# Normalised operand splits, convolutions read from PSUM, batched attention sums and a new planner clock rule in a two-layer hybrid encoder

## The chip, the cores and the metric

The kernel runs as one program on one core of a Trainium2 chip. The metric is the device time of one execution in microseconds (us); lower is better. Engines are named as in the profile: PE is TensorE (matmuls), DVE is VectorE, ACT is ScalarE, POOL is GpSimd and SP issues the DMAs. PSUM is the memory that PE writes, in eight banks of 128x512 float32; SBUF holds everything else.

## The reference

What is computed is an encoder of two layers on 512 tokens of width 1024, all in float32:

```python
def reference(x, positions, norm_mix, w_in, ...):
    for l in range(DEPTH):
        h = rms_norm(x, norm_mix[l])
        proj = h @ w_in[l]
        aq, ak, av, dqkv, dz, dalpha, dbeta, rwp = _split(proj, IN_SPLITS)
        y_att = attention_mixer(aq, ak, av, positions, attn_sink[l])
        y_dn = deltanet_mixer(dqkv, dz, dalpha, dbeta, dn_conv[l], dn_a_log[l],
                              dn_dt_bias[l], dn_norm[l])
        y_rw = rwkv_mixer(rwp, rw_mu[l], rw_w0[l], rw_w_up[l], ...)
        mixed = jnp.concatenate([y_att, y_dn, y_rw], axis=-1)
        x = x + mixed @ w_out[l]
        h = rms_norm(x, norm_ffn[l])
        x = x + conv_ffn(h, ffn_w_up[l], ffn_conv[l], ffn_w_down[l])
    return rms_norm(x, norm_final)
```

`rms_norm` divides each token by the root mean square of its 1024 values and multiplies by a gain. The attention mixer has six query heads, two key/value heads, a window of 128 tokens to either side, a rotation of part of each head (rope) and a sink per head. The DeltaNet mixer runs a width-5 convolution along the tokens, then a chunked recurrence with a triangular inverse in each of the two directions. The RWKV mixer mixes each token with its two neighbours (token shift) and runs a chunked recurrence in both directions. `conv_ffn` is a gated feed-forward net with a width-3 convolution between its two products.

## The kernel before

Activations lie transposed: 128 features in the partitions, 512 tokens along a row, so that x is eight tiles of 128x512. Every large product is made in a split form: a float32 operand a is written as ah + al, both in PE's faster 32-bit type, and `product` (line 738) issues three matmuls for each of the eight k-tiles: wh by xh, wh by xl and wl by xh. A projection is thus 24 matmuls of 512 columns into one PSUM bank. For its weights `weights` loads four k-tiles at a time by DMA into `wr`, ACT casts them into `wh`, and POOL subtracts, `wl` = `wr` - `wh`.

A layer has a mixer part with 26 projections: eight for RWKV, one for the DeltaNet gates, nine for the DeltaNet convolutions, three for its output gates, and K, V and three Q for attention. Around them stand `rwkv_prep` (twice), `invert` (a forward substitution on 32x32 blocks, 30 dependent steps on DVE), `finish_inverse`, `rwkv_scan` (eight steps), `dn_prep` (three times), `invert_both` (30 steps on DVE), `dn_scan` (eight steps), three attention heads, `rwkv_out` and `dn_out`. Then follow the output projection `w_out`, the feed-forward up-products (44 tiles) and the down-products (eight tiles of 22 k-tiles).

The norm is put in late. `split` takes x times its gain only, and the factor of each token, 1/rms, lies as a row tile `rb` (128x512). Each consumer multiplies the projection's PSUM result by `rb`: `token_shift` (line 889), `dn_conv` (line 1103), `dn_gates`, `rope`, the V tile and `gate_proj`. In `dn_conv` that multiplication also moves the result from PSUM into an SBUF tile `td`; four DVE instructions then add the shifted taps, reading `td`:

```python
V.tensor_tensor(u, o, rb, mult)
S.activation(dst, u, AF.Copy, scale=w(2))
```

An attention head works through four blocks of 128 queries, and in each on two groups: scores, maximum, exponential, the sum `den`, its reciprocal, a scaling, transposes and the product with V. The small instructions (`es`, `nmx`, `den`) are 128x2 in size, once in each block.

The order of all work is decided when the program is built. The class `Plan` records each instruction with its price and its dependencies; `schedule` then runs a list scheduler over the five engines, in which an instruction's priority is the longest path behind it plus a lead for its task from the table `LEAD` (37 numbers, the same for both layers). Some instructions have an alternative engine (`other`, line 268): copies may go to ACT or DVE, though not those that write the matmul's split type. The program is emitted in the order of the planned starts, and all of its instructions carry the line of that one call, L516. An instruction waits on the chip for its operands, and the queue behind it waits with it.

## Time and profile before

| what | us |
|---|---|
| median of three runs | 1678.78 |
| the three runs | 1677.74 to 1680.12 |
| the profiled execution, its own time | 1681.65 |
| its span | 1679.5 |
| PE busy | 1531.1 |
| DVE busy | 1083.1 |
| ACT busy | 736.2 |
| POOL busy | 645.2 |
| mixer part of layer 0 (from the first matmuls to the end of `dn_out`) | 13 to 434 |
| `w_out` of layer 0 | 434 to 480 |
| feed-forward part of layer 0 | 480 to 840 |
| the same three of layer 1 | 840 to 1260, 1260 to 1306, 1306 to 1664 |

The page gives each engine's busy time, the granted clock of PE in 40 slices, the chain of work that ended last, and groups of instructions by shape. The busy time of PE has to be read with care: matmul records overlap, and a matmul that runs at the lower clock lasts longer. Because every instruction carries the same line, the groups are told apart by tile names and shapes: `td`, `tr` and `cv` are working tiles in SBUF, `ps` is PSUM, `hh` and `hl` are the two halves of an activation, `wh` and `wl` those of a weight, `rb` is the norm's factor and `fixed` holds constants and parameters.

### The profile page before, as it was taken

To read this page: it belongs to the slowest core of one execution; us is meant where nothing else is said; L and a number is where in the kernel's file an instruction comes from. 1 tells how busy PE (TensorE), PEld (TensorE's weight loads), DVE (VectorE), ACT (ScalarE), POOL (GpSimd) and SP (SyncE) were. 2 spreads that over 40 slices of the span, in tenths; PEclk is the share of its full clock that TensorE was granted. 3 is DMA by queue.
4 is the path that set the end of the run, shared out by engine and by line. 5 is a ranking of instruction groups with operands and counts; after the bars stand their busy time and mean duration, and the time that the engine had idled before them with its cause. 6 is when DMAs were issued, how large, how long until landed. Compare 5 with 4: busy or idle time off the path is not lost. (4 is left out here: it accounts for less than half of the span.)

```text
span 1679.5 us, 29012 instructions
## 1 busy us (share of the span) xinstructions
PE 1531.1 (91%) x11500; PEld 1192.8 (71%) x11500; DVE 1083.1 (64%) x1689; ACT 736.2 (44%) x1399; POOL 645.2 (38%) x510
## 2 busy tenths in 40 slices
PE   7999787589999999999999996966899999999996
PEld 5677665367777777788876775644677877777885
DVE  7799977967437666740058998789654566766101
ACT  5565345454543433332236544355544433334221
POOL 5422332010555554555552232410017454555553
PEclk9999889779999999999999997996799999999998
DMA  6312303010233333333342121120003333333332
GB/s 177 84 34 76 70 20 89 13 34 2 71 91 100 94 89 95 94 106 112 108 105 64 47 75 39 54 86 1 27 14 89 94 88 95 95 93 88 115 91 85
DMA packets 230536, 126.07 MB, mean 75 GB/s; under 512 B 23656, under 2 KB 221416, under 8 KB 230400
## 3 DMA queue, kind: packets, MB, share of 16 engines
q1 hardware_dynamic: 228624, 121.02, 25.8%
q10 hardware_dynamic: 1776, 3.20, 0.7%
q8 instruction: 90, 1.47, 0.3%
q14 instruction: 46, 0.38, 0.1%
HBM read 117.84 MB, written 6.34 MB: 74 GB/s over the span
## 5 line engine op out<-in xcount | busy, mean ns | idle before, releaser
L516 POOL TENSOR_TENSOR wl<-wr,wh 128x512 fp32r<-128x512 f32 (+1 forms) x408 | 558.1, 1379 | 830.1 <-ACT wh L516 667.9
L516 PE MATMUL ps<-hh,wh 128*128 128x512 f32 x1248 | 457.6, 399 | 6.9 <-ACT wh L516 6.9
L516 ACT ACTIVATE wh<-wr 128x512 fp32r<-128x512 f32 (+1 forms) x408 | 243.5, 616 | 495.9 <-PE ps L516 433.9
L516 PE MATMUL ps<-hh,wl 128*128 128x512 f32 x1248 | 452.9, 398 | 7.4 <-POOL wl L516 5.3
L516 PE MATMUL ps<-hl,wh 128*128 128x512 f32 x1248 | 451.6, 394 | 0.0
L516 PEld LDWEIGHTS ps<-hh,wl 128*128 128x128 f32 x1248 | 232.7, 187 | 84.2 <-POOL wl L516 30.3
L516 PEld LDWEIGHTS ps<-hh,wh 128*128 128x128 f32 x1248 | 233.6, 188 | 69.8 <-ACT wh L516 16.2
L516 PEld LDWEIGHTS ps<-hl,wh 128*128 128x128 f32 x1248 | 233.8, 188 | 51.7 <-issue 3.4
L516 DVE TENSOR_TENSOR p<-ps,p 128x512 f32<-128x512 f32 (+2 forms) x72 | 38.2, 551 | 197.4 <-PE ps L516 197.1
L516 PE MATMUL ps<-p,wh 128*128 128x512 f32 x512 | 158.2, 389 | 0.0
L516 DVE TENSOR_TENSOR td<-ps,rb 128x512 f32<-128x512 f32 (+1 forms) x64 | 43.7, 688 | 136.4 <-PE ps L516 136.3
L516 PEld LDWEIGHTS ps<-p,wh 128*128 128x128 f32 x512 | 96.1, 188 | 19.9
L516 DVE SCALAR_TENSOR_TENSOR tr<-td,fixed,tr 128x511 f32<-128x511 f32 x88 | 105.3, 1197 | 0.6 <-ACT tr L516 0.4
L516 PE MATMUL ps<-p,wl 128*128 128x512 f32 x256 | 99.8, 390 | 0.0
L516 ACT ACTIVATE p<-p 32x256 f32<-32x256 f32 (+3 forms) x112 | 66.0, 589 | 16.1 <-DVE p L516 11.2
L516 PE MATMUL ps<-fixed,cv 128*128 128x128 f32 x168 | 36.6, 338 | 38.8 <-ACT cv L516 35.7
L516 DVE SCALAR_TENSOR_TENSOR td<-tr,fixed,td 128x511 f32<-128x511 f32 x88 | 70.8, 805 | 0.3
L516 PE MATMUL ps<-p,p 32*32 32x32 f32 (+2 forms) x1232 | 56.1, 253 | 14.9 <-DVE p L516 11.3
L516 DVE TENSOR_TENSOR tr<-tr,td 128x512 f32<-128x512 f32 x44 | 67.3, 1529 | 1.6
L516 ACT ACTIVATE p<-ps 64x256 f32<-64x256 f32 (+4 forms) x113 | 44.9, 401 | 52.7 <-PE ps L516 33.3
L516 PEld LDWEIGHTS ps<-sm,p 64*64 64x64 f32 x1344 | 49.4, 145 | 24.6 <-DVE sm L516 12.9
L516 PEld LDWEIGHTS ps<-p,p 32*32 32x32 f32 (+1 forms) x1232 | 51.3, 143 | 21.5 <-DVE p L516 12.1
(170 smaller groups left out, 2089.5 us busy)
## 6 DMA issues: line engine op xcount, KB each, us to landing
wr<-ffn_w_up SPq DMA_DIRECT2D x176, 256.0 KB, 2.8
wr<-w_in SPq DMA_DIRECT2D x88, 256.0 KB, 2.8
wr<-ffn_w_down SPq DMA_DIRECT2D x80, 256.0 KB, 2.9
p<-scr ACTq DMA_DIRECT2D x12, 256.0 KB, 5.1
wr<-w_in SPq DMA_DIRECT2D x24, 128.0 KB, 2.6
wr<-w_out SPq DMA_DIRECT2D x32, 96.0 KB, 2.6
wr<-w_out SPq DMA_DIRECT2D x16, 192.0 KB, 2.6
p<-xt SPq DMA_DIRECT2D x8, 256.0 KB, 4.5
```

What stands on the lines that cost most here:

```text
L516: tc.keep_in_program_order(call(*args, **kw))
```

## The change

The eight RWKV projections keep the late norm, now applied in place in PSUM. After each of them `renorm` makes one k-tile of the normalised input (x times gain times `rb`, on DVE) and splits it anew into `gh` and `gl`; all other 18 projections of the mixer take this split, and their consumers lose the multiplication by `rb`. `dn_conv` reads its taps from PSUM. `rope` makes its scaled copy on ACT and both products on DVE, and `gate_proj` takes its sigmoid from PSUM. An attention head now holds all eight score tiles and makes `es`, `nmx`, `den` and the reciprocal once, at 128x8; its parts have leads of their own. In the planner, casts that write the split type may move from ACT to DVE, and products and sums of two SBUF tiles may move between DVE and POOL; the `LEAD` table has an entry for each task in each layer; and the rule by which the planner prices PE's clock is another. The feed-forward code is as it was, and so is the number of instructions on PE.

```diff
...
@@ LEAD @@
-    "attn_head0": -17500, "attn_head1": 13500, "attn_head2": 4300, ...
...
@@ def other @@
-        if not self.flexible or not writes or len(reads) < 1 or "float32r" in str(writes[0].dtype) or reads[0].dtype != F32:
+        if not writes or not reads:
             return None
...
+        if name == "tensor_tensor" and not psum and n >= 128 and len(dst.shape) == 2 and o.eng in ("DVE", "POOL"):
+            e, f, cost = ("POOL", self.nc.gpsimd, 180 + 2.3 * n) if o.eng == "DVE" else ("DVE", self.nc.vector, 165 + 1.04 * n)
+            return e, f.tensor_tensor, o.args, o.kw, cost
...
@@ def split @@
-        hi = plan.tile(bp, [P, T], F32R, tag=f"hh{k}", bufs=2, name=nm("hh"))
+        hi = plan.tile(bp, [P, T], F32R, tag=f"{tag}h{k}", bufs=1, name=nm(tag + "h"))
...
@@ def token_shift @@
-        u = t2("r")
+        u = o
         V.tensor_tensor(u, o, rb, mult)
...
@@ def dn_conv @@
-    def dn_conv(l, o, i, rb, dst):
-        u = t2("d")
-        V.tensor_tensor(u, o, rb, mult)
+    def dn_conv(l, u, i, dst):
...
@@ def rope @@
-        V.scalar_tensor_tensor(q, o, scale, rb, mult, mult)
+        S.activation(q, o, AF.Copy, scale=scale)
+        V.scalar_tensor_tensor(dst, o, scale, cos_t, mult, mult)
         pr = ps("r")
         PE.matmul(pr, C("rot"), q, start=True, stop=True)
-        V.tensor_tensor(dst, pr, sin_t, mult)
-        G.tensor_tensor(q, q, cos_t, mult)
+        V.tensor_tensor(q, pr, sin_t, mult)
         V.tensor_tensor(dst, dst, q, add)
...
@@ def attn_head @@
+        V.tensor_tensor(den, den, es, add)
+        V.reciprocal(den, den)
+        po = ps("r")
...
@@ def layer @@
+        def renorm(k):
+
+            xn = t2("d")
+            V.scalar_tensor_tensor(xn, x[k], norm.g[:, k : k + 1], rb, mult, mult)
+            normed.append(split(xn, None, "g", k))
...
-            o = proj(l, parts, COL_RW + P * i)
+            o = proj(l, parts, COL_RW + P * i, st="jjod"[i % 4])
...
+            renorm(i)
...
+        parts = normed
...
-            V.tensor_tensor(z, o, rb, mult)
-            sigmoid(sg, z)
-            V.tensor_tensor(z, z, sg, mult)
+            sigmoid(sg, o)
+            V.tensor_tensor(z, o, sg, mult)
...
-                o = proj(l, parts, COL_DQKV + P * i)
+                o = proj(l, parts, COL_DQKV + P * i, st="o" if i == pr_ < 2 else "j")
                 dst = cv()
-                dn_conv(l, o, i, rb, dst)
+                dn_conv(l, o, i, dst)
...
```

What the planner makes of it is shown at three places, each before and after. The first is DVE at the first DeltaNet convolutions of layer 0, behind `rwkv_prep` (`cv` is a convolution's result, `td` the normalised copy). Before:

```order
98 L516 TENSOR_TENSOR td_254<-ps_246,rb_75 128x512
99 L516 TENSOR_TENSOR td_264<-ps_256,rb_75 128x512
100 L516 SCALAR_TENSOR_TENSOR p_276<-fixed,p_276 128x512
101 L516 SCALAR_TENSOR_TENSOR cv_253<-td_254,fixed,cv_253 128x510
102 L516 COPY fixed<-ps_245 128x8x6
103 L516 SCALAR_TENSOR_TENSOR cv_263<-td_264,fixed,cv_263 128x510
104 L516 SCALAR_TENSOR_TENSOR cv_253<-td_254,fixed,cv_253 128x511
105 L516 SCALAR_TENSOR_TENSOR cv_263<-td_264,fixed,cv_263 128x511
106 L516 SCALAR_TENSOR_TENSOR cv_253<-td_254,fixed,cv_253 128x511
107 L516 SCALAR_TENSOR_TENSOR cv_263<-td_264,fixed,cv_263 128x511
108 L516 SCALAR_TENSOR_TENSOR cv_253<-td_254,fixed,cv_253 128x510
109 L516 SCALAR_TENSOR_TENSOR cv_263<-td_264,fixed,cv_263 128x510
```

After:

```order
111 L547 TENSOR_SCALAR cv_278<-ps_271,fixed 128x512
112 L547 TENSOR_TENSOR p_221<-ps_247,fixed 128x512
113 L547 SCALAR_TENSOR_TENSOR cv_278<-ps_271,fixed,cv_278 128x510
114 L547 SCALAR_TENSOR_TENSOR cv_278<-ps_271,fixed,cv_278 128x511 x2
115 L547 SCALAR_TENSOR_TENSOR cv_278<-ps_271,fixed,cv_278 128x510
116 L547 SCALAR_TENSOR_TENSOR p_289<-fixed,p_289 128x512
117 L547 CAST wh_339<-wr_338 128x512
118 L547 SCALAR_TENSOR_TENSOR td_260<-fixed,td_260 12x512
119 L547 TENSOR_TENSOR cv_278<-cv_278,td_279 128x512
```

The copies into `td` (rows 98 and 99 of before) are gone, the taps read `ps`, and a weight cast stands among them (row 117), which ACT did before.

The second place is PE at the end of `dn_scan` in layer 0 (`sm` is the scan's state and vectors, `hh` and `hl` with `wh` the first matmuls of `w_out`, `at` with `at` the scores of attention, `tr` with `at` its product with V). Before:

```order
1193 L516 MATMUL ps_799<-sm_798,p_388 64x64 x4
1194 L516 MATMUL ps_799<-sm_798,p_529 64x64 x4
1195 L516 MATMUL ps_799<-sm_798,p_544 64x64 x4
1196 L516 MATMUL ps_815<-p_383,sm_779 64x64 x2
1197 L516 MATMUL ps_815<-p_385,sm_797 64x64 x2
1198 L516 MATMUL ps_850<-hh_828,wh_852 128x512
1199 L516 MATMUL ps_861<-hh_828,wh_863 128x512
1200 L516 MATMUL ps_813<-sm_800,cv_253 64x64 x4
1201 L516 MATMUL ps_813<-sm_800,cv_331 64x64 x4
1202 L516 MATMUL ps_813<-sm_800,cv_398 64x64 x4
1203 L516 MATMUL ps_815<-p_524,sm_779 64x64 x2
```

After:

```order
1186 L547 MATMUL ps_752<-p_548,sm_751 64x64 x2
1187 L547 MATMUL ps_771<-at_443,at_515 128x256
1188 L547 MATMUL ps_772<-at_443,at_515 128x256
1189 L547 MATMUL ps_791<-td_790,fixed 128x512
1190 L547 MATMUL ps_821<-hh_799,wh_823 128x512
1191 L547 MATMUL ps_832<-hh_799,wh_834 128x512
1192 L547 MATMUL ps_821<-hl_800,wh_823 128x512
1193 L547 MATMUL ps_832<-hl_800,wh_834 128x512
1194 L547 MATMUL ps_821<-hh_799,wl_824 128x512
1195 L547 MATMUL ps_832<-hh_799,wl_835 128x512
1196 L547 MATMUL ps_794<-td_793,fixed 128x512
1197 L547 MATMUL ps_797<-td_796,fixed 128x512
1198 L547 MATMUL ps_703<-tr_718,at_463 64x128
1199 L547 MATMUL ps_703<-tr_720,at_463 64x128
1200 L547 MATMUL ps_703<-tr_718,at_463 64x128
```

Before, 16 matmuls of `w_out` stand among the scan's last matmuls and another 16 beside `dn_out`, and no attention work is left by then. After, none stands inside the scan and six beside `dn_out`; behind them come the last attention head's remaining 20 transposes and 34 products with V (rows 1198 on), and the rest of `w_out` after those.

The third place is DVE in the up-products of layer 0's feed-forward part. Before:

```order
641 L516 TENSOR_TENSOR td_1028<-ps_1021,rb_848 128x512
642 L516 TENSOR_TENSOR tr_1018<-ps_1011,rb_848 128x512
643 L516 TENSOR_SCALAR td_1019<-tr_1018,fixed 128x512
644 L516 SCALAR_TENSOR_TENSOR tr_1029<-td_1028,fixed,tr_1029 128x511
645 L516 SCALAR_TENSOR_TENSOR td_1019<-tr_1018,fixed,td_1019 128x511
646 L516 SCALAR_TENSOR_TENSOR tr_1029<-td_1028,fixed,tr_1029 128x511
647 L516 SCALAR_TENSOR_TENSOR td_1019<-tr_1018,fixed,td_1019 128x511
648 L516 TENSOR_TENSOR tr_1010<-tr_1010,td_1019 128x512
649 L516 TENSOR_TENSOR p_1020<-tr_1010,p_1020 128x512
```

After:

```order
699 L547 CAST p_1067<-tr_1057 128x512
700 L547 TENSOR_TENSOR p_1067<-tr_1057,p_1067 128x512
701 L547 CAST wh_1101<-wr_1100 128x512
702 L547 CAST wh_1108<-wr_1107 128x512
703 L547 TENSOR_TENSOR td_1094<-ps_1087,rb_819 128x512
704 L547 TENSOR_TENSOR tr_1084<-ps_1077,rb_819 128x512
705 L547 SCALAR_TENSOR_TENSOR tr_1095<-td_1094,fixed,tr_1095 128x511
706 L547 SCALAR_TENSOR_TENSOR td_1085<-tr_1084,fixed,td_1085 128x511
707 L547 SCALAR_TENSOR_TENSOR tr_1095<-td_1094,fixed,tr_1095 128x511
708 L547 SCALAR_TENSOR_TENSOR td_1085<-tr_1084,fixed,td_1085 128x511
709 L547 TENSOR_TENSOR tr_1076<-tr_1076,td_1085 128x512
710 L547 CAST p_1086<-tr_1076 128x512
```

The work on `ps` and `td` is the same, and casts of weights (`wh`) and of the result (`p` from `tr`), which ACT made before, now stand between: 41 weight casts and 14 others in each layer's up-products.

## Rows read from the trace of the kernel before

**Rows 1.** The page's parts 1 and 2: busy time of each engine; granted clock in tenths.

```profile
PE 1531.1 (91%) x11500; PEld 1192.8 (71%) x11500; DVE 1083.1 (64%) x1689; ACT 736.2 (44%) x1399; POOL 645.2 (38%) x510
...
PEclk9999889779999999999999997996799999999998
```

**Rows 2.** Busy time by stretch (us; x is instructions), then granted clock, DMA share, GB/s.

```profile
13.00:73.00 60.00, 57.51 (x237) 41.62 (x238) 45.98 (x55) 28.45 (x53) 29.00 (x21) 1.00 0.41 105
80.00:146.00 66.00, 61.83 (x815) 50.21 (x813) 61.18 (x86) 43.99 (x89) 13.75 (x8) 1.00 0.20 54
146.00:203.00 57.00, 46.15 (x309) 37.18 (x303) 54.81 (x85) 21.62 (x40) 22.24 (x17) 0.90 0.32 75
203.00:210.00 7.00, 5.42 (x140) 4.80 (x140) 4.91 (x12) 4.35 (x11) 0.00 (x0) 0.50 0.01 2
210.00:265.00 55.00, 49.03 (x686) 37.18 (x687) 39.00 (x74) 19.95 (x38) 20.28 (x27) 0.92 0.11 27
265.00:298.00 33.00, 24.36 (x231) 16.20 (x231) 28.29 (x48) 21.70 (x43) 2.50 (x5) 0.90 0.37 94
298.00:346.00 48.00, 29.59 (x125) 18.15 (x123) 44.92 (x102) 20.26 (x59) 2.59 (x3) 0.72 0.04 11
362.00:380.00 18.00, 15.63 (x224) 11.61 (x221) 9.02 (x30) 7.10 (x20) 1.68 (x2) 0.70 0.11 39
480.00:740.00 260.00, 257.44 (x1108) 205.95 (x1107) 172.16 (x198) 101.69 (x160) 132.02 (x93) 1.00 0.32 92
```

**Rows 3.** Groups of DVE instructions by shape: busy us, mean ns, then idle before.

```profile
L516 DVE SCALAR_TENSOR_TENSOR cv<-td,fixed,cv 128x511 f32<-128x511 f32 x36 | 30.9, 885 | 0.7
...
L516 DVE SCALAR_TENSOR_TENSOR p<-tr,fixed,p 128x511 f32<-128x511 f32 x32 | 30.4, 952 | 1.3 <-ACT p L516 0.4
...
L516 DVE SCALAR_TENSOR_TENSOR cv<-td,fixed,cv 128x510 f32<-128x510 f32 x36 | 27.8, 785 | 1.8 <-ACT cv L516 1.4
...
L516 DVE TENSOR_TENSOR td<-ps,rb 128x512 f32<-128x512 f32 x62 | 42.4, 689 | 136.4 <-PE ps L516 136.3
...
L516 DVE TENSOR_TENSOR cv<-cv,td 128x512 f32<-128x512 f32 x24 | 23.8, 1006 | 5.8 <-ACT td L516 5.7
...
L516 DVE TENSOR_SCALAR td<-tr,fixed 128x512 f32<-128x512 f32 x40 | 21.8, 544 | 1.4
...
L516 DVE TENSOR_TENSOR p<-p,tr 128x512 f32<-128x512 f32 x18 | 13.2, 739 | 1.3 <-ACT tr L516 0.7
...
L516 DVE SCALAR_TENSOR_TENSOR p<-p,fixed,rb 128x512 f32<-128x512 f32 x8 | 5.4, 745 | 5.6 <-ACT rb L516 5.6
...
L516 DVE TENSOR_TENSOR es<-fixed,mx 128x2 f32<-128x2 f32 x24 | 4.6, 191 | 0.7
```

**Rows 4.** DVE beside POOL in the feed-forward stage: start us, duration us, engine, operation.

```profile
617.74 0.51 DVE L516 TENSOR_SCALAR td<-tr,fixed 128x512 f32<-128x512 f32 x1
618.17 1.78 DVE L516 SCALAR_TENSOR_TENSOR tr<-td,fixed,tr 128x511 f32<-128x511 f32 x1
619.87 0.74 DVE L516 SCALAR_TENSOR_TENSOR td<-tr,fixed,td 128x511 f32<-128x511 f32 x1
...
616.66 2.73 POOL L516 TENSOR_TENSOR wl<-wr,wh 128x512 fp32r<-128x512 f32 x2 [0.47 <-PE ps L516]
```

**Rows 5.** DVE at four steps of the DeltaNet scan, layer 0, same columns as rows 4.

```profile
367.65 0.56 DVE L516 TENSOR_TENSOR sm<-ps,fixed 128x384 f32<-128x384 f32 x1 [3.04 <-PE ps L516]
...
380.32 0.55 DVE L516 TENSOR_TENSOR sm<-ps,fixed 128x384 f32<-128x384 f32 x1
...
408.52 0.56 DVE L516 TENSOR_TENSOR sm<-ps,fixed 128x384 f32<-128x384 f32 x1 [0.16 <-PE ps L516]
...
414.26 0.56 DVE L516 TENSOR_TENSOR sm<-ps,fixed 128x384 f32<-128x384 f32 x1 [1.11 <-PE ps L516]
```

**Rows 6.** PE, attention work between steps of the same scan, same columns as rows 4.

```profile
405.73 0.66 PE L516 MATMUL ps<-fixed,cv 128*128 128x128 f32 x4
406.32 1.31 PE L516 MATMUL ps<-tr,at 128*64 128x128 f32 x14
```

More of the change, by code (lines that the diff above doesn't have):

```diff
@@ L120 @@
 LEAD = {
[6 rows of a table removed]
-    "token_shift": 631900,
[20 rows of a table added]
 }
@@ L273, in other @@
         n = int(np.prod(dst.shape[1:]))
-        psum = str(src.space).endswith("PSUM")
+        psum = any(str(x.space).endswith("PSUM") for x in reads + writes)
         if o.eng == "ACT" and name == "activation" and o.args[2] == AF.Copy and set(o.kw) <= {"scale"}:
@@ L329, in price @@
         return n
-    SWITCH, STAY, COLD, WARM = 150, 300, 5000, 4000
+    SWITCH, STAY = 150, 300
+    BEAT, DOWN, UP = 3413.0, 0.44, 0.8
+    WEIGHT = {"full": 1.0, "half": 0.8, "q64": 0.9, "q32": 0.2}
     def admit(self, t):
@@ L385, in schedule @@
         avail = {e: [] for e in engines}
-        last, cold, heat, dma_free, releases = None, False, 0.0, 0.0, []
+        last, slow, here, then, edge, lit, dma_free, releases = None, False, 0.0, 0.0, self.BEAT, 0.0, 0.0, []
         push, pop = heapq.heappush, heapq.heappop
@@ L405, in wake @@
         def wake(r, t):
-            for h, e in held[r]:
-                push(heaps[e], (max(t, h.ready), h.n))
-            held[r] = []
+            was, held[r] = held[r], []
+            for h, e in was:
+                if h.done:
+                    continue
+                still = blocked(h)
+                if still is None:
+                    push(heaps[e], (max(t, h.ready), h.n))
+                else:
+                    held[still].append((h, e))
         order = []
@@ L483, in schedule @@
                 last = o.mode
-                if t - free[e] > self.COLD:
-                    cold, heat = True, 0.0
-                if cold:
+                while t >= edge:
+                    slow = here < (self.UP if slow else self.DOWN) * self.BEAT
+                    here, then, edge = then, 0.0, edge + self.BEAT
+                if slow:
                     cost *= 2
-                    heat += cost if o.mode == "full" else 0
-                    cold = heat < self.WARM
-            elif o.contend and e == "DVE" and free["POOL"] > t:
+                w, a, b = self.WEIGHT[o.mode], max(t, lit), t + cost + 150
+                if b > a:
+                    here += w * max(0.0, min(b, edge) - a)
+                    then += w * max(0.0, b - max(a, edge))
+                    lit = b
+            elif e == "DVE" and (o.contend or o.eng == "POOL") and free["POOL"] > t:
                 cost += min(cost, free["POOL"] - t)
@@ L1299, in attn_head @@
     def attn_head(l, tq, q, k, vt, dst):
[L1300 to L1304 removed]
+        span = [(max(0, nb - 1), min(3, nb + 1) + 1) for nb in range(4)]
+        scs = [[cv() for g in range(2)] for nb in range(4)]
+        mxt, nmx, es, den = (tiny(8, tag=tag) for tag in ("mx", "nmx", "es", "den"))
+        by = lambda a: a.rearrange("p (n g) -> p n g", g=2)
+        for nb, (k0, k1) in enumerate(span):
+            W = P * (k1 - k0)
             m0 = P * (k0 - nb + 1)
[L1306 to L1307 removed]
             for g in range(2):
@@ new lines, in attn_head @@
+        yield
+        V.tensor_tensor(by(es), sinkb[l][:, tq : 6 : 3].unsqueeze(1).broadcast_to([P, 4, 2]), by(mxt), sub)
+        V.tensor_scalar(nmx, mxt, -1.0, None, mult)
+        S.activation(es, es, AF.Exp)
+        for nb, (k0, k1) in enumerate(span):
+            W = P * (k1 - k0)
+            for g in range(2):
+                u = slice(2 * nb + g, 2 * nb + g + 1)
+                S.activation(scs[nb][g][:, :W], scs[nb][g][:, :W], AF.Exp, bias=nmx[:, u], accum_out=den[:, u])
+        yield
```

76 lines of the change are left out of this document (32 added, 44 removed), and 26 rows, old and new, of the table LEAD.

## The prediction

> **What bounds the kernel now.** I first read the page's busy times and the granted clock in slices [rows 1], then busy time by stretch [rows 2], then the DVE groups by shape [rows 3], then single instructions at three places [rows 4 to 6]. The chain of waits is no help here, as it covers only the end of the run. PE is busy 91% of the span [rows 1], but the stretches differ. In the feed-forward stretch, PE works 257.44 of 260 us at full clock while DVE works 172.16 [rows 2]: PE sets that time, and 257.44 us over 1108 instructions is 0.232 us for one split matmul. The first projections (13 to 73) are alike, PE 57.51 of 60. In the mixer it is DVE that is full: 61.18 of 66 us, 54.81 of 57, and 44.92 of 48 in the last forward substitution [rows 2]. PE looks busy beside it, but its clock stands at 0.90, 0.72 and 0.70 of full in these stretches, that is, part of the time at 1.2 instead of 2.4 GHz. It lies low after PE had little to do: in 298 to 346 PE works 29.59 of 48 us. In the two scans, short steps run from PE to DVE and back, and nothing is full. So a microsecond taken from PE in the mixer is worth little, one taken from DVE much, and in the feed-forward part neither DVE nor ACT matters until one reaches PE's time.
>
> **The change, part by part.** I laid the two orders of DVE side by side, cut them at the same tasks, and priced each instruction at its mean in this trace. In layer 0 and layer 1 this gives, before and after: `rwkv_prep` with the first convolutions 67.0 to 64.8 and 68.1 to 59.1; `invert` to `finish_inverse0` 58.9 to 58.0 and 58.3 to 55.9; `rwkv_scan` with `dn_prep` 75.7 to 60.4 and 75.2 to 64.3; `invert_both` with its `finish_inverse` 60.9 to 58.1 and 60.9 to 59.9; `dn_scan` 44.4 to 34.8 and 44.4 to 33.9; the end up to `dn_out` 5.8 to 11.9 and 5.8 to 15.5.
>
> Where this comes from, per layer: nine multiplications by `rb` into `td` fall away, 9 x 0.689 = 6.2 us [rows 3], and four of V and the gates. The 36 taps of the convolutions go from 0.885 and 0.785 [rows 3] to reading PSUM, where the 0.689 of `td<-ps,rb` is the nearest row: 36 x 0.146 = 5.3. The 16 token shifts save 16 x (0.952 - 0.689) = 4.2. Nine sums `cv<-cv,td` at 1.006 and nine `p<-p,tr` at 0.739 go to POOL (15.7). Nine in twelve of each tiny attention instruction go; `es` at 0.191 is the row for them. Added are eight `renorm` (nearest row `p<-p,fixed,rb`, 0.745: 6.0), three `gl`, some 18 weight casts and up to 13 copies from PSUM of half width. For the cast the trace has no row on DVE; the nearest is the copy with a scale, `td<-tr,fixed`, 0.544 [rows 3], so 18 x 0.544 = 9.8. Bounds for a cast: 0.51 [rows 4] below, 1.78, a fully held instruction in rows 4, above. I take 0.544, as a cast has the same one input.
>
> By stage, what of this lies on the path:
>
> First projections: PE is the bound; `renorm` and its splits add some 10 us to DVE's 45.98 of 60 [rows 2], less the 4.2 of token shift. Hidden: 0. Without that cover it would cost the 10.
>
> 80 to 146, DVE full: -2.2 in layer 0, -9.0 in layer 1. A convolution now holds its PSUM bank for five reads instead of one, 3.4 us instead of 0.7. The next projection needs 24 x 0.232 = 5.6 us in another bank, which covers that: 0, at worst 2.7 for each of nine.
>
> 146 to 210, DVE full: -0.9 and -2.4. In layer 1 the fill of split matmuls (97 instead of 175 during `invert`) leaves 26 for the inside of `finish_inverse0`, a 7 us stretch at clock 0.50 with PE at 5.42 [rows 2]; at full clock half of that goes: -2.5 in layer 1, bounds 0 and -2.7 each.
>
> 210 to 298: DVE loses 15.3 and 10.9, but it was busy only 39.00 of 55 and 28.29 of 33 us, and PE 49.03 and 24.36 [rows 2]. PE receives K, V and Q projections that stood elsewhere: by counts, 8.1 us more work in layer 0 and 15.5 in layer 1. The next late thing is PE. Bounds are -15.3 and +8.1 (layer 1: -10.9 and +15.5); I take -2.5 and 0, near PE's side, since the waits between engines remain.
>
> 298 to 362, DVE nearly full: -2.8 and -1.0, from the attention pieces leaving the gaps between substitution steps.
>
> `dn_scan`: the `t1` instructions of DVE mark the steps, at 367.65, 380.32, 408.52 and 414.26 [rows 5]. The first step shown takes 12.7 us, the last 5.7, and from 367.65 to 414.26 there are six steps in 46.6 us. The long one carries attention work on both engines at clock 0.70 (362 to 380, [rows 2]). With DVE's 44.4 at 34.8 and one attention head out of the way, I set all steps to 6.3: 37.8 instead of 46.6, -8.8 in each layer. Bounds 0 and -12 (all at 5.7).
>
> After the scan: before, 32 matmuls of `w_out` were done by the end of `dn_out`, now 6. The other 26 come later, 26 x 0.232 = +6.0 in each layer; beside `dn_out` now stands the end of the last head: 20 transposes at 0.66 / 4 and 34 products at 1.31 / 14 [rows 6], 6.5 us of PE. That is cover of the same size as the matmuls were, and not a second cost. Bounds 0 and +14, if the head's chain through DVE and ACT outlasts it.
>
> Feed-forward: 59 more casts on DVE in each layer, 59 x 0.544 = 32, so 172.16 becomes 204 of 257 [rows 2]. ACT is relieved and was not the bound. 0.
>
> The sum is -11.2 in layer 0 (-2.2 -0.9 -2.5 -2.8 -8.8 +6.0) and -17.7 in layer 1 (-9.0 -2.4 -2.5 -1.0 -8.8 +6.0), together -28.9. The profiled execution took 1681.65, which gives 1652.7. The median lies 2.87 below that execution, so I forecast 1650.
>
> **One rule against this change.** In rows 4 POOL works on two `wl` from 616.66 to 619.39. The scaled copy on DVE at 617.74 takes 0.51 all the same, while the instruction with two SBUF inputs at 618.17 takes 1.78, ending after POOL does, and its like at 619.87 takes 0.74. So an input from PSUM or one SBUF input goes free, and two are held. The Trainium skill, page "SBUF — State Buffer", section "Who interferes with whom", says that a DVE instruction with two SBUF inputs contends with POOL's reads, and the trace agrees (0.74 against 1.78). It also says that copies, casts and scaled copies can take both ports and then contend; the 0.51 does not show that here. By that rule a cast would be held like the 1.78 above.
>
> **The rivals.** *Slower: POOL holds DVE.* POOL gets 24 more two-input instructions per layer, in the stretches where DVE is full. Each can hold a two-input instruction of DVE, 1.78 - 0.74 = 1.04 us [rows 4]: 48 x 1.04 = 50 us in all. On top, if casts are held as well, the feed-forward DVE stands at 172 + 41 x 1.5 + 18 x 0.544 = 243, near PE's 257, with order waits on weights perhaps 4 us per layer. The forecast's 28.9 is lost when 0.6 of each possible hold occurs; at all of them the time is 1650 + 50 = 1700. For it: the 1.006 of `cv<-cv,td`, against 0.739 for `p<-p,tr`, shows holds in the mixer already. Against it: POOL works only 13.75 of 66 us and 2.50 of 33 in these stretches [rows 2], so most new work falls where nobody is held, and the taps now read PSUM and cannot be held. 0.17.
>
> *Same: PE takes back what DVE gives.* If the projections moved into 210 to 298 are not covered, this stage costs +8.1 and +15.5 instead of -2.5 and 0: 1650 + 26 = 1676. For it: PE's 49.03 of 55 us. Against it: a fifth of PE's time there is at the lower clock. 0.11.
>
> *Much faster: the clock stays up.* By rows 2 the time at the lower level in layer 0 is twice the missing share: 11 of 57 us, 7 of 7, 9 of 55, 7 of 33, 27 of 48, 11 of 18, together 72 us. If the moved fill keeps PE working and half of this time hangs on PE, each layer saves a further 72 / 2 / 2 = 18: 1650 - 36 = 1614. For it: PE gets more fill under `invert_both` (58 and 72 split matmuls of the gates). Against it: in `invert` it gets less, and under the substitutions the path is DVE's. 0.12.
>
> **How the numbers follow.** The forecast has 0.60; its own range is 1626 (all of DVE's saving in 210 to 298 counts) to 1668 (the head's chain outlasts `dn_out`, and 210 to 298 gives nothing). The rivals take 0.17 at 1682 to 1702, 0.11 at 1668 to 1681 and 0.12 at 1600 to 1625. A measurement of this kernel tells about 0.2% from no change, that is 1675.4 to 1682.1. Faster is 0.60 + 0.12 + half of the 0.11 = 0.77; same is the other half, 0.06; slower 0.17. From 1610 to 1690 about half of the two outer rivals is left out, so the range holds some 0.85.
>
> **What would show it.** Right: steps of `dn_scan` near 6.3 us from the first on; DVE's taps at 0.69 from PSUM; casts on DVE near 0.55; the feed-forward stretch unchanged at 257 of 260; `rwkv_prep` to `invert` shorter by some 9 us in layer 1 and hardly in layer 0. Wrong: two-input DVE instructions in the mixer at 1.2 us and more with POOL busy beside them; casts at 1 us; PE gaps in the up-products; 210 to 298 longer than 88 us; a tail behind `dn_scan` of more than 14 us before `w_out` runs through.

## The result and the profile after

The change made the kernel slower: 1752.51 us (median of four runs, 1752.08 to 1752.97) against 1678.66 for the kernel before on the same chip, a ratio of 1.0439 [1.0421, 1.0457]. The forecast was 1650, faster, and the time lies outside its range and above the top of the slower rival. The profiled execution took 1752.19, its span is 1750.4.

The page of after, busy time by engine and the granted clock of PE in tenths over 40 slices, answers to [rows 1]:

```profile
PE 1550.9 (89%) x11500; PEld 1190.5 (68%) x11500; DVE 1258.6 (72%) x1891; ACT 563.1 (32%) x1081; POOL 704.5 (40%) x558
...
PEclk9998879859999999999999898996799999999999
```

PE has the same 11500 instructions. ACT lost 173 us of work, DVE gained 175 and POOL 59.

The span was then cut at the same task ends in both traces. In each column layer 0 stands ahead of layer 1; the difference is after minus before, all in us:

| stretch | before L0, L1 | after L0, L1 | difference |
|---|---|---|---|
| start of the layer to the end of the last-started RWKV projection | 66.2, 50.4 | 75.4, 50.7 | +9.2, +0.3 |
| to the end of `rwkv_prep` | 82.7, 83.2 | 90.7, 88.7 | +8.0, +5.5 |
| `invert` and `finish_inverse0` | 61.5, 61.8 | 60.9, 51.9 | -0.6, -9.9 |
| `rwkv_scan` up to the start of `invert_both` | 87.1, 86.2 | 88.1, 88.8 | +1.0, +2.6 |
| `invert_both` with `finish_inverse1` and `2` | 64.4, 64.6 | 72.7, 72.9 | +8.3, +8.3 |
| `dn_scan` | 62.7, 63.1 | 51.6, 52.5 | -11.1, -10.6 |
| end of `dn_scan` to the last matmul of `w_out` | 43.2, 43.3 | 61.8, 61.6 | +18.6, +18.3 |
| up-products | 262.8, 259.5 | 272.3, 271.3 | +9.5, +11.8 |
| down-products | 111.3, 110.4 | 112.2, 112.2 | +0.9, +1.8 |

With -1.6 for the end of the program, the differences add up, within rounding, to the 70.5 us between the ends of the last computing instruction, 1676.0 and 1746.5. Four things are to be explained: the up-products, the stretch behind `dn_scan`, the early mixer with the start, and `invert_both` with its inverse. One RWKV projection, the fourth by number, isn't inside the first row: in after its last matmuls stand in the second stretch, ending at 131.9 in layer 0, where they ended at 70.7 before.

Busy time by stretch of the kernel after, layer 0, columns as in [rows 2]: `rwkv_prep`, the half-clock part of `invert_both`'s end, then `dn_scan`, the attention tail, `w_out` and the up-products:

```profile
75.40:166.10 90.70, 80.13 (x821) 57.73 (x819) 74.89 (x104) 56.45 (x101) 21.13 (x14) 0.91 0.16 42
...
371.50:387.80 16.30, 12.60 (x344) 11.11 (x344) 5.74 (x14) 3.22 (x8) 0.00 (x0) 0.50 0.01 3
388.00:439.40 51.40, 47.78 (x934) 37.52 (x934) 31.12 (x95) 17.55 (x47) 7.49 (x8) 0.95 0.01 3
439.40:455.50 16.10, 14.52 (x107) 10.93 (x104) 12.19 (x26) 13.22 (x35) 4.18 (x3) 1.00 0.00 1
455.50:501.20 45.70, 43.41 (x186) 33.82 (x185) 26.28 (x33) 7.98 (x14) 26.42 (x20) 1.00 0.30 86
501.20:773.50 272.30, 257.63 (x1101) 202.31 (x1100) 218.23 (x260) 63.23 (x99) 128.18 (x97) 1.00 0.31 89
```

The same stretches of the kernel before, cut at its own task ends:

```profile
66.20:148.90 82.70, 78.47 (x876) 59.72 (x874) 76.86 (x104) 59.19 (x114) 20.66 (x14) 1.00 0.21 56
351.20:361.80 10.60, 8.09 (x262) 7.63 (x263) 7.31 (x19) 7.08 (x16) 1.27 (x1) 0.55 0.23 56
361.80:424.50 62.70, 58.38 (x1022) 45.62 (x1019) 39.16 (x121) 27.28 (x79) 5.04 (x6) 0.91 0.04 13
424.50:433.90 9.40, 9.31 (x36) 6.32 (x35) 6.16 (x9) 7.19 (x12) 2.96 (x2) 1.00 0.20 56
433.90:467.70 33.80, 33.80 (x148) 27.12 (x147) 13.53 (x16) 15.23 (x26) 23.27 (x17) 1.00 0.32 91
467.70:730.40 262.70, 258.20 (x1100) 205.55 (x1099) 170.04 (x195) 104.73 (x165) 134.27 (x95) 0.99 0.32 93
```

In the up-products PE has the same work (257.63 and 258.20 us), yet the stretch grew by 9.6: PE now waits 14.7 us, where it waited 4.5. DVE is busy 218 of 272, so it isn't full either. Work of the last two attention heads and more of `w_out` now stand behind the scan, as the order said: 107 and 186 PE instructions in the two stretches, where there were 36 and 148, and PE is nearly full in all of them.

DVE groups of after by shape, columns as in [rows 3]:

```profile
L547 DVE CAST wh<-wr 128x512 fp32r<-128x512 f32 x203 | 135.8, 670 | 249.6 <-PE ps L547 218.0 <-DMA wr<-ffn_w_down 15.0 <-issue 12.6
...
L547 DVE TENSOR_TENSOR p<-tr,p 128x512 fp32r<-128x512 f32 x30 | 31.2, 1041 | 1.3
...
L547 DVE SCALAR_TENSOR_TENSOR cv<-ps,fixed,cv 128x511 f32<-128x511 f32 x36 | 26.2, 746 | 0.7
L547 DVE SCALAR_TENSOR_TENSOR cv<-ps,fixed,cv 128x510 f32<-128x510 f32 x36 | 25.9, 741 | 0.5
L547 DVE SCALAR_TENSOR_TENSOR td<-p,fixed,rb 128x512 f32<-128x512 f32 x16 | 23.4, 1518 | 2.3 <-ACT rb L547 2.3
L547 DVE TENSOR_SCALAR td<-tr,fixed 128x512 f32<-128x512 f32 x15 | 21.5, 1433 | 0.5
```

The convolution taps that read PSUM take 0.746 and 0.741, as a whole and with POOL busier than before; they were 0.885 and 0.785 [rows 3]. A free instruction of the same kind with both inputs in SBUF takes 0.74 too [rows 4], so reading PSUM takes the holds away and doesn't make the tap itself faster; the forecast had 0.689. What reads SBUF got dearer: the scaled copy `td<-tr` went from 0.544 [rows 3] to 1.433, the sum `p<-tr,p` from 0.692 to 1.041, `renorm` (`td<-p,fixed,rb`) 1.518 where 0.745 was forecast, and the mean cast 0.670.

How PE comes to wait in the up-products is seen at 599 to 612 us of after. DVE's timeline, start and duration in us:

```profile
599.41 1.62 DVE L547 TENSOR_SCALAR td<-tr,fixed 128x512 f32<-128x512 f32 x1
...
603.43 0.43 DVE L547 CAST p<-tr 128x512 fp32r<-128x512 f32 x1
603.89 1.67 DVE L547 TENSOR_TENSOR p<-tr,p 128x512 fp32r<-128x512 f32 x1
605.49 1.55 DVE L547 CAST wh<-wr 128x512 fp32r<-128x512 f32 x1
...
609.45 0.68 DVE L547 TENSOR_TENSOR tr<-ps,rb 128x512 f32<-128x512 f32 x1
```

POOL, ACT and PE at the same place, same columns; in brackets the idle time ahead of an instruction and what ended it:

```profile
598.20 2.55 POOL L547 TENSOR_TENSOR wl<-wr,wh 128x512 fp32r<-128x512 f32 x2 [2.94 <-PE ps L547]
603.71 1.31 POOL L547 TENSOR_TENSOR wl<-wr,wh 128x512 fp32r<-128x512 f32 x1 [2.96 <-PE ps L547]
605.46 1.29 POOL L547 TENSOR_TENSOR wl<-wr,wh 128x512 fp32r<-128x512 f32 x1 [0.45 <-issue]
...
610.17 0.72 ACT L547 ACTIVATE td<-tr,fixed 128x512 f32<-128x512 f32 x1 [6.19 <-DVE tr L547]
610.82 0.63 ACT L547 ACTIVATE tr<-tr 128x512 f32<-128x512 f32 x1
611.36 0.61 ACT L547 ACTIVATE wh<-wr 128x512 fp32r<-128x512 f32 x1
...
612.02 0.50 PE L547 MATMUL ps<-hh,wh 128*128 128x512 f32 x1 [1.42 <-ACT wh L547]
```

The cast at 603.43 starts while POOL is idle and takes 0.43; the one at 605.49 runs beside a `wl` and takes 1.55, and so does the scaled copy at 599.41 (1.62). These are single-input instructions. The prediction read the 0.51 in [rows 4] as a sign that they go free; that row lies across the seam between POOL's two `wl` (616.66 + 2.73 / 2 = 618.03), so at most 0.3 us of it ran beside the first. POOL's pair took 2.73 there and 2.55 at 598.20, so it was POOL that waited a little. The Trainium skill, page "SBUF — State Buffer", section "Who interferes with whom", has it right: copies, casts and scaled copies can take both ports and then contend with POOL. Then the chain: ACT's weight cast at 611.36 has its input, but stands in ACT's queue behind a scaled copy that waits 6.19 us for `tr` of DVE, which DVE starts at 609.45 because it had a held sum (603.89) and a held cast (605.49) ahead of it; and PE waits 1.42 us for that `wh`.

Who PE waits for in this stretch, of after (total us, times, longest):

```profile
PE ps L547 <- ACT wh L547: 8.5, 6, 1.5
PE ps L547 <- DVE wh L547: 5.4, 8, 0.9
PE ps L547 <- POOL wl L547: 0.6, 1, 0.6
```

The largest part is not DVE's casts but the casts that ACT kept.

### The profile page after: what moved, and what is told of

Its sections match the earlier page's. It is cut to its first block, busy times and chain, and to the rows that moved or that the text cites. A ratio compares the mean times of both kernels' runs of the same rounds, so it can differ in the third digit from the quotient of the medians.

```text
span 1750.4 us, 28839 instructions
## 1 busy us (share of the span) xinstructions
PE 1550.9 (89%) x11500; PEld 1190.5 (68%) x11500; DVE 1258.6 (72%) x1891; ACT 563.1 (32%) x1081; POOL 704.5 (40%) x558
## 5 line engine op out<-in xcount | busy, mean ns | idle before, releaser
L547 PE MATMUL ps<-hh,wh 128*128 128x512 f32 x960 | 365.1, 399 | 34.2 <-ACT wh L547 17.6
L547 PE MATMUL ps<-hh,wl 128*128 128x512 f32 x960 | 353.2, 397 | 5.4 <-POOL wl L547 5.2
L547 PE MATMUL ps<-hl,wh 128*128 128x512 f32 x960 | 355.8, 393 | 0.1
L547 DVE CAST wh<-wr 128x512 fp32r<-128x512 f32 (+1 forms) x221 | 142.9, 648 | 276.2 <-PE ps L547 244.6
L547 ACT ACTIVATE wh<-wr 128x512 fp32r<-128x512 f32 x187 | 116.1, 625 | 531.6 <-PE ps L547 484.2
L547 PEld LDWEIGHTS ps<-hl,wh 128*128 128x128 f32 x960 | 180.6, 188 | 37.6 <-DVE hl L547 1.3
L547 PE MATMUL ps<-gh,wh 128*128 128x512 f32 (+1 forms) x288 | 115.8, 420 | 3.5 <-ACT wh L547 2.9
L547 PE MATMUL ps<-gh,wl 128*128 128x512 f32 (+1 forms) x288 | 114.2, 415 | 2.6 <-POOL wl L547 2.5
L547 PE MATMUL ps<-gl,wh 128*128 128x512 f32 (+1 forms) x288 | 112.3, 407 | 0.0
L547 PEld LDWEIGHTS ps<-gh,wh 128*128 128x128 f32 (+1 forms) x288 | 54.8, 191 | 25.2 <-issue 6.0
```

What stands on the lines that cost most here:

```text
L547: tc.keep_in_program_order(call(*args, **kw))
```

## The experiments

Where did the 21 us of the two up-products come from, and what of the mixer's 50? The first four kernels split the planner's new freedom: weight casts on DVE, sums on POOL. In the first three the order of after stays as it is, and an instruction is put back on its old engine only when it is emitted. The runs were made on four chips, each beside the kernel before (medians of 1678 to 1683 us); a ratio is to that kernel's time there.

**Casts back on ACT.**

```diff
-            call, args, kw = (o.call, o.args, o.kw) if o.run == o.eng else o.alt[1:4]
+            split = "float32r" in str(getattr(o.args[0], "dtype", "")) and o.call.__name__ == "activation"
+            call, args, kw = (o.call, o.args, o.kw) if o.run == o.eng or split else o.alt[1:4]
```

> The changed kernel in its own order, except that every cast into the matmul's split type that the planner gave to DVE (221 weight casts and some 60 of activations) is issued on ACT, as before. Theory (casts on DVE are held by POOL, lengthen DVE's queue in the feed-forward part and make PE wait for weights): the two feed-forward stretches with w_out, 23 and 19 us longer than before the change, come back to within 6 us each, and the start and the mixers give some 10 more, 1752 to about 1700 (1690 to 1715). Rival (the planner's new order and the early renorm cost the time, not the engine of the casts): above 1735.

Measured 1750.19, ratio 1.0428 [1.0402, 1.0455]: within the uncertainty of after's own. The up-products take 268.4 and 267.8, 4 us less in each layer, not the 10 to 12 that were lost. The theory missed, and the rival's 1735 and above held: in this order, which engine casts is the smaller part.

**Sums and products back on their own engine.**

```diff
+            pair = o.call.__name__ == "tensor_tensor"
+            call, args, kw = (o.call, o.args, o.kw) if o.run == o.eng or pair else o.alt[1:4]
```

> The changed kernel in its own order, except that every sum or product of two SBUF tiles that the planner moved between DVE and POOL is issued on its old engine (POOL loses about 24 in each layer). The rival of the prediction (POOL's added sums hold DVE at about 1 us each, 50 us in all): about 1705 to 1720. Theory (casts and renorm are what costs; the moved sums lie where POOL had room): 1735 to 1755, the feed-forward stretches unchanged within 3 us.

Measured 1758.34, 1.0476 [1.045, 1.0503], up-products 272.3 and 270.6. In this order POOL's added sums are not the cause: taken back to DVE, they give nothing.

**Both.** The two edits together.

> Both of the above: casts on ACT, sums on their old engines, order as in the changed kernel. If the two act by the same holds, the gain is that of casts alone plus 5 to 15: about 1690. If it stays above 1735, what the planner may place on which engine is not the cause, and it is in the order or in renorm.

Measured 1755.43, 1.0456 [1.0425, 1.0486]; up-products 268.1 and 267.0. With every choice of the new rule undone, none of the whole loss is gone, and of the 21 us in the two up-products 13 are still there. The feed-forward code and its engines are then those of before, so these 13 lie in the order.

**The planner without that freedom.** Here `other` refuses both, and a new order is made.

```diff
-        if not writes or not reads:
+        if not writes or not reads or name == "tensor_tensor" or "float32r" in str(writes[0].dtype):
             return None
```

> The changed kernel with the planner itself forbidden to move split casts and sums of two SBUF tiles, so that it plans a new order for these engines (its table of leads was not made for that). Theory: the feed-forward stretches as before the change (458 and 416 us), the whole 1675 to 1705. Rival (the order by the new table and clock rule costs the time): above 1730, with feed-forward stretches still 15 us or more longer.

Measured 1749.69, 1.0422 [1.0397, 1.0447]. The up-products are 259.9 in both layers, as before the change; the mixers got worse by nearly as much (the second row of the table is 104.1 us in layer 0, 90.7 in after), so the whole missed its 1675 to 1705. I read this so: the `LEAD` table belongs to an order, and another rule makes another one from it.

**The change without its planner**, that is, the new computation planned by the old class with the old 37 leads (the RWKV, DeltaNet and attention code of after, `Plan` and `LEAD` of before).

> The changed computation (normalised split, convolutions from PSUM, batched attention sums) on the planner of before: its engine rules, its clock rule and its 37 leads. Theory (the new order costs the time, the computation is worth about what was forecast): the feed-forward stretches at 458 and 416 us, the mixers 5 to 15 us shorter than before, 1650 to 1680. Rival (the computation itself costs: renorm on DVE beside POOL at the start, PSUM banks held by the convolutions): 1700 or more, with the first 66 us grown by 8 or more in each layer.

Measured 1814.08, 1.0779 [1.0761, 1.0797]. The up-products take 261.2 and 257.6, but `dn_scan` 76.6 and 76.8 and `finish_inverse0` 26.2 and 26.5. The rival's 1700 or more held, but not at its place: the first row of the table grew by 7.7 and 0.2 us. The old leads don't fit the new computation, as I read it; whether the computation alone costs can't be told from this run.

**The kernel before with only the new choice of engines** (`other` and its price for a held instruction):

```diff
-        if not self.flexible or not writes or len(reads) < 1 or "float32r" in str(writes[0].dtype) or reads[0].dtype != F32:
+        if not writes or not reads:
             return None
...
+        if name == "tensor_tensor" and not psum and n >= 128 and len(dst.shape) == 2 and o.eng in ("DVE", "POOL"):
```

> The kernel before with only the planner's engine rule of the change: split casts may go to DVE, sums of two SBUF tiles to POOL or back; clock rule and leads as before. Theory (in the feed-forward part this rule makes an order in which casts, epilogues and POOL's subtractions block each other): 20 us more in each feed-forward stretch, some in the mixers, 1710 to 1740. Rival (the loss needs the new leads or clock rule): within 10 us of before, 1670 to 1690.

Measured 1761.96, 1.0469 [1.0446, 1.0492]. The up-products are 271.7 and 271.6, those of after, with none of the new computation in the kernel. Layer 0, columns as in [rows 2], and who PE waits for there:

```profile
497.80:769.50 271.70, 257.21 (x1101) 202.51 (x1100) 218.62 (x260) 63.85 (x99) 127.44 (x96) 1.00 0.32 90
...
PE ps L519 <- ACT wh L519: 8.5, 6, 1.4
PE ps L519 <- DVE wh L519: 5.3, 8, 0.9
```

These are nearly the numbers of after, 218.23 of DVE and waits of 8.5 and 5.4 among them. So the loss there comes from this rule. No task of the feed-forward part has an entry in `LEAD`, so leads old or new don't enter its priorities. The mixers, which have them, lose 35 and 33 us too.

**The kernel before with the whole new planner** (its clock rule as well) and the old leads.

> The kernel before on the whole new planner (engine rule and clock rule) but with the 37 old leads. Against the run with the engine rule alone, the difference is the clock rule: theory none within 10 us in the feed-forward part, where the clock is full; in the mixers up to 20 either way. If it is near 1750 the planner's rules alone make the loss.

Measured 1758.44, 1.0447 [1.043, 1.0465], up-products 271.7 and 271.5. The new price of the clock moves the time by less than the two intervals can tell apart.

**Every second weight cast outside the mixers on DVE**, in the order of the kernel before, 152 casts:

```diff
+            if o.group is None and o.eng == "ACT" and "float32r" in str(getattr(o.args[0], "dtype", "")) and o.args[0].tensor.name.startswith("wh"):
+                self.turns = getattr(self, "turns", 0) + 1
+                if self.turns % 2:
+                    call, args, kw = self.nc.vector.tensor_copy, o.args[:2], {}
```

> The kernel before in its own order, with every second weight cast outside the mixers (about 150) issued on DVE instead of ACT. If casts on DVE cost by themselves (held by POOL, epilogues behind them), 1700 to 1720; if an order made for ACT takes them without loss, since DVE has time there (172 of 260 us busy), 1675 to 1690, and the loss in the changed kernel lies in its order.

Measured 1698.75, 1.0087 [1.0072, 1.0103]; up-products 267.5 and 268.5, that is, 5 and 9 us more than before. This lies between the two expectations, at the edge of the first. The disputed cost by itself: casts on DVE are not free, though DVE has room on the page. The mean cast takes 0.551 here.

**The rule off outside the mixers only.** The mixers are planned by the rules of after; only instructions outside a mixer task keep their engine.

```diff
+        if self.group is None and (name == "tensor_tensor" or "float32r" in str(writes[0].dtype)):
+            return None
```

> The changed kernel with the planner's new engine rule switched off for work outside the mixers' tasks: w_out, feed-forward, norms, renorm and its splits. The mixers keep it, and the leads and clock rule are those of the change. Theory (the rule makes the order in which the up-products' casts, epilogues and subtractions block each other): the up-products take 260 us in each layer instead of 272.3 and 271.3, and the whole 1725 to 1735, with the mixers within 5 us. Rival (the loss there comes with the new clock rule or from what the mixers leave behind): up-products above 268, the whole above 1745.

Measured 1714.37, 1.0197 [1.0172, 1.0221]: about 38 us of the 74 are gone (41 by the ratios), more than expected, since the mixers moved by more than 5 us. Windows of this kernel, `w_out` and the up-products of layer 0:

```profile
447.60:490.50 42.90, 42.15 (x181) 33.47 (x182) 12.52 (x15) 17.45 (x30) 25.73 (x19) 1.00 0.31 89
490.50:752.10 261.60, 257.69 (x1101) 204.64 (x1100) 170.06 (x196) 104.50 (x165) 135.70 (x96) 1.00 0.32 93
```

Its DVE groups, same columns as above:

```profile
L549 DVE TENSOR_TENSOR p<-tr,p 128x512 fp32r<-128x512 f32 x32 | 22.2, 693 | 22.8 <-ACT p L549 22.8
...
L549 DVE TENSOR_SCALAR td<-tr,fixed 128x512 f32<-128x512 f32 x40 | 20.3, 508 | 1.4
...
L549 DVE SCALAR_TENSOR_TENSOR td<-p,fixed,rb 128x512 f32<-128x512 f32 x16 | 17.8, 1126 | 0.0
L549 DVE CAST wh<-wr 128x512 fp32r<-128x512 f32 x34 | 17.7, 526 | 61.1 <-PE ps L549 55.2 <-issue 5.7
```

The stretch is 261.6 long with DVE at 170, and the scaled copy is back at 0.508, the sum `p<-tr,p` at 0.693 and the cast at 0.526. So here the rule made the up-products longer. Of the 38 us they are 22; among the rest are the first projections (75.4 to 71.2) and `dn_scan` (51.6 to 47.9).

**`renorm` taken off DVE** in after's order: its 16 products become copies on ACT with a constant factor, so that the gain and the norm's factor are left out.

```diff
+            if o.call.__name__ == "scalar_tensor_tensor" and o.args[0].tensor.name in self.plain:
+                call, args, kw = self.nc.scalar.activation, (o.args[0], o.args[1], AF.Copy), {"scale": 0.05}
```

> The changed kernel in its own order, but the 16 products of renorm are issued on ACT as a copy with a constant scale. The gain and the norm's factor are left out of the normalised split, so this output is not the reference's. Theory (renorm on DVE, held by POOL at 1.5 us each, delays the first token shifts): the first projections end at 68 to 70 us instead of 75.4 and rwkv_prep1 7 us or more earlier; the whole 1738 to 1747. Rival (the start is late because of the order of casts and splits): less than 3 us at that place.

Measured 1747.81, 1.0391 [1.0364, 1.0418]. The first row of the table ends at 74.2 instead of 75.4, and `rwkv_prep` at 165.1 instead of 166.1. DVE of this run, ahead of its first token shift:

```profile
31.20 1.83 DVE L550 TENSOR_TENSOR gl<-td,gh 128x512 fp32r<-128x512 f32 x1 [8.35 <-ACT gh L550]
```

DVE now idles for 8.35 us, and the token shift still starts at 35.43, behind this `gl`, which waits for ACT's `gh`. So the holds on `renorm` are not what delays the start; the place of the split in DVE's queue remains, and no run changed that alone.

**Both of the last two.**

> Both edits of the two runs above (the second leaves the norm's factor and gain out of the split, so the output is not the reference's). If they act at different places the gains add: about 1715 to 1728, and what remains above 1679 lies in the mixers: the tail of attention behind the DeltaNet scan (some 7 us in each layer after what the scan saves) and finish_inverse at half clock (5 us in each layer).

Measured 1709.84, 1.0167 [1.0145, 1.019]; the first row ends at 69.4. The whole is below the expected range because the kernel without the `renorm` edit already was. Against that kernel, on the same chip, it is 4.5 us less; against after the `renorm` edit alone gave 4.7 by the medians and 8 by the ratios. So the gains add as far as these runs can tell, and the intervals are wider than the gain.

**Work for PE behind the forward substitutions.** `finish_inverse1` and `2` run at clock 0.50, the 1.2 GHz level, after the substitution. 44 matmuls without use, 128x384, were put behind its last eleven steps, into the kernel with the rule off outside the mixers.

```diff
+            if o.n in self.warm:
+                out, w, x = self.warm[o.n]
+                tc.keep_in_program_order(self.nc.tensor.matmul(out, w, x, start=True, stop=True))
...
+            if 20 <= j < 31:
+                plan.warm[len(plan.ops) - 1] = ...
```

> The kernel with the engine rule off outside the mixers, with 44 extra matmuls (128 by 384 float32, their results unused) on PE, one behind each of the last 11 steps of every forward substitution, in the emitted order and with nothing else moved. Theory (finish_inverse is slow because PE idled through the substitution and stands at half clock): the stage behind invert_both falls from 16.0 to about 10 us in each layer, the first scan steps gain a little, the whole 1714 to 1698 to 1704. Rival (the stage is bound by its copies on ACT and DVE, or the extra matmuls delay the chain): 1710 to 1722.

Measured 1724.54, 1.0256 [1.0237, 1.0274]. The stage still ran at 0.50 and took 16.0 us, so nothing follows for the clock.

**The same matmuls in the kernel before.**

> The kernel before with the same 44 extra matmuls. Theory: finish_inverse0 falls from 12.5 to about 9 us, the stage behind invert_both from 10.7 to about 8, the first DeltaNet steps from 12.7 towards 7 us; the whole 1665 to 1674, faster than both kernels. Rival: within 4 us of 1680, or slower if a late extra matmul stands ahead of finish_inverse.

Measured 1704.13, 1.0134 [1.0116, 1.0152]. Two windows of this run, the end of the substitution and the stage behind it:

```profile
350.00:365.00 15.00, 15.00 (x151) 9.75 (x152) 11.30 (x15) 7.61 (x17) 1.29 (x1) 1.00 0.00 1
364.00:376.10 12.10, 9.36 (x344) 8.45 (x343) 7.41 (x20) 8.78 (x21) 1.27 (x1) 0.67 0.23 63
```

Here the clock did rise, to full ahead of the stage and 0.67 in it (0.55 before the change), and the stage still took 12.1 us where it took 10.6. But it holds 344 PE instructions, where it held 262, as some of the inverse's work had slipped behind the extra matmuls. Its like is the stage of after, with 344 as well and, but for three, the same shapes: 16.30 us at 0.50 with PE busy 12.60, against 12.10 at 0.67 with PE busy 9.36. That speaks for the lower clock as part of the cost; the two kernels differ in more than the clock, so it isn't shown by itself. The edit's own price was visible: the substitutions went from 49.0 to 55.1, 53.7 to 60.3 and 53.9 to 61.3 us. I put this down to DVE's next step waiting for the added readers of its tile, which no run separates.

## Why the prediction was wrong, step by step

**Feed-forward, 0: the step that failed first, +10.4 and +13.6 with the down-products.** It let 204 us of DVE hide under PE's 257. DVE came to 218 (the casts at 0.670 and held epilogues, not 0.544), still under 272, so the sum of busy times was nearly right and the conclusion wrong. Busy share is no cover when the queues are in order: a weight cast on DVE stands behind the epilogue, an epilogue copy on ACT stands ahead of the next weight cast, both wait for POOL's holds, and PE waits for the weight. PE waited 14.7 us of the stretch, where it had waited 4.5. The kernel with the rule off outside the mixers (261.5 and 260.4) and the kernel before with the rule on (271.7 and 271.6) settle that the rule does it. Two parts of it were separated: moving casts alone costs 5 to 9 in the order of before, putting them back in after's order gives 4. The rest lies in the order that the rule makes. The prediction's slower rival had the right neighbour (held casts) but sized it at 4 us a layer.

**The rule of the Trainium skill that I set aside** was the right one, for the reason shown at 603 to 605 us. I had one row for the single-input instruction, and didn't ask where it stood between POOL's two. The two means (0.544 before, 1.433 after) depend on how many of the copies a POOL instruction held. Yet a price of a held cast would not have been enough, as the casts put back on ACT show.

**First projections, 0: measured +9.2 in layer 0.** DVE at the start of after:

```profile
19.06 5.14 DVE L547 SCALAR_TENSOR_TENSOR td<-p,fixed,rb 128x512 f32<-128x512 f32 x3
...
25.82 6.89 DVE L547 SCALAR_TENSOR_TENSOR td<-p,fixed,rb 128x512 f32<-128x512 f32 x4
...
36.79 1.28 DVE L547 TENSOR_TENSOR ps<-ps,rb 128x512 f32<-128x512 f32 x2
```

Seven `renorm` products, each held at 1.7, and the splits `gl` on DVE and POOL run ahead of the first token shift, which starts at 36.79 instead of 24.58; the first split matmul starts at 17.44 instead of 12.81. My 10 us of DVE "hidden under PE" were put into the queue ahead of what PE's PSUM banks wait for. Taking the products off DVE gave 1.2 us, with DVE idle ahead of a `gl`, so their holds are not the cost, and the order of the splits and casts remains: with the rule off outside the mixers 4.2 us of the 9.2 came back. The other 5 stay open. In layer 1, where the same terms were hidden too, it was +0.3.

**80 to 146, -2.2 and -9.0: measured +8.0 and +5.5** from the end of the RWKV projections to the end of `rwkv_prep`. DVE's work did fall, from 76.86 to 74.89, and the taps got cheaper, though to 0.74 and not 0.689. But the stretch is 8 us longer with DVE no longer full and the clock at 0.91, where it was 1.00. The step that failed was to turn work taken off the fullest engine into time. This stays at 8 us in the kernel with the rule off, and no run separates its cause. In the trace of after, 99.9 to 106.7 and 134 to 144.2 lie at clock 0.50, with PE busy 5.84 and 7.18 us in them; an estimate from these is 6.5 us at full clock. Ahead of the second, PE waits 4.1 us for `td`. There also lies the late RWKV projection, its last matmul and the start of its token shift:

```profile
131.50 0.40 PE L547 MATMUL ps<-hh,wl 128*128 128x512 f32 x1
...
135.86 0.70 DVE L547 TENSOR_TENSOR ps<-ps,rb 128x512 f32<-128x512 f32 x1
```

Before, that projection ended at 70.7. Its lateness isn't enough as a cause: in the change without its planner it ends at 57.3, and the stretch is longer still, about 99 us.

**146 to 210, -0.9 and -4.9: measured -0.6 and -9.9.** The direction held, and layer 1 gave more. **210 to 298, -2.5 and 0: measured +1.0 and +2.6.** PE took back what DVE gave, as that rival had it, at a small part of its price.

**298 to 362, -2.8 and -1.0: measured +8.3 and +8.3.** 2.7 of it are in the substitution and 5.6 in `finish_inverse1` and `2`, which have 344 PE instructions at clock 0.50 in 16.30 us, where 262 at 0.55 filled 10.60 before. Work that had run within the substitution moved behind it. Beside the kernel before with extra matmuls (12.10 us at 0.67 for the same count), both have a part in the 5.6: the moved work, and the lower clock under it. How they share it is open.

**`dn_scan`, -8.8: measured -11.1 and -10.6**, within its bounds. Eight steps in 51.6 us are 6.4 each, against 62.7 / 8 = 7.8 before; the forecast set 6.3, but took the gain of six steps alone. Reading attention's work out of the long steps in [rows 5] was right.

**After the scan, +6.0: measured +18.6 and +18.3**, above the upper bound of 14. PE of after in the tail, same columns as [rows 6]:

```profile
443.77 2.24 PE L547 MATMUL ps<-tr,at 128*64 128x128 f32 x24
...
449.54 2.08 PE L547 MATMUL ps<-fixed,cv 128*128 128x128 f32 x16
451.55 3.33 PE L547 MATMUL ps<-tr,at 128*64 128x128 f32 x32
454.81 0.73 PE L547 MATMUL ps<-hh,wh 128*128 128x512 f32 x2
```

I said that the head's transposes and products were "cover of the same size as the matmuls were, and not a second cost". They were a cost: PE is busy 14.52 of the 16.10 us of this tail, and the rest of `w_out` starts behind these rows, at 454.81. By count the two stretches behind the scan hold 107 + 186 = 293 PE instructions, where they held 36 + 148 = 184. PE's work over the scan and these two is 58.38 + 9.31 + 33.80 = 101.5 us before and 47.78 + 14.52 + 43.41 = 105.7 after, in 105.9 and 113.2 us. What left the scan is PE work on a PE that is nearly full, and it costs its length behind the scan: the scan gave 11.1 and the tail took 18.6. The failed step was to price the scan by its steps and the tail by its matmuls, when both draw on one budget of PE. With the rule off outside the mixers the three stretches take 108.3 us, so 2.4 remain of the 7.3. That is a reading of the traces; no run moved the head back by itself.

**The clock** did not stay up, as the third rival had it: it fell from 1.00 to 0.91 in `rwkv_prep` and from 0.55 to 0.50 in the stage of `finish_inverse1` and `2`, and rose from 0.91 to 0.95 in the scan.

**The whole.** The two layers were to change by -28.9 us. Measured against forecast, both layers together, the terms that missed most are the feed-forward part (+24.0 for 0), the tail behind the scan (+36.9 for +12.0), `rwkv_prep` (+13.5 for -11.2), `invert_both` with its inverse (+16.6 for -3.8) and the start (+9.5 for 0). Of the 74 us between the medians, the rule for instructions outside the mixers accounts for about 38, shown by a run. The other 36 are in the mixers; in the kernel with that rule off the larger pieces are `rwkv_prep` (+8 in each layer), `invert_both` with its inverse (+7 and +8) and the start (+5), less 7 at `invert` of layer 1. Whether the computation or the order made for it is to blame there stays open: apart from the kernel with the rule off outside the mixers, every kernel that was planned anew with leads made for something else came out at 1750 to 1814 (ratios 1.042 to 1.078), so none of them is a clean test of the computation. No kernel of this study beat the one before.

## What to carry to other kernels

An engine's spare time hides added work only if that work stands at the right place of its queue; before costing a moved instruction at nothing, read what is queued behind it and which in-order queue waits for that. When work leaves a stretch, follow it to where it lands, and add up the engine that is nearly full over both. A table of leads is worth tens of microseconds and belongs to the prices and the choices it was made for, so where the table has entries, a planner's rule can't be judged by an old one.

## What was not expected of the hardware

A cast of 128x512 on DVE took 0.43 when it began with POOL idle and 1.55 beside POOL's subtraction, and the scaled copy 0.508 (mean with the rule off) and 1.62: a factor of about three for single-input instructions with SBUF operands. Beside such POOL work the taps from PSUM stayed at their free time. Four of them and POOL, after:

```profile
122.93 3.10 DVE L547 SCALAR_TENSOR_TENSOR cv<-ps,fixed,cv 128x510 f32<-128x510 f32 x4
...
122.96 1.28 POOL L547 TENSOR_TENSOR cv<-cv,td 128x512 f32<-128x512 f32 x1 [20.46 <-ACT td L547]
124.18 1.31 POOL L547 TENSOR_TENSOR wl<-wr,wh 128x512 fp32r<-128x512 f32 x1
```

POOL's two took their free time as well (1.29 and 1.31 at 605.46 and 603.71).
